# Decay matrices from differences of running sums, adaLN vectors of the first FFN by ScalarE products and GpSimd sums, and B kept once

## The chip, the cores and the metric

The kernel runs on one core of a Trainium2 chip. The metric is device microseconds of one execution; smaller is better.

## What is computed

The program is a block of two layers over 512 latent tokens and 256 context tokens of width 1024. Layer 0 runs grouped-query attention and a bidirectional Mamba-2 scan (SSD) side by side, layer 1 is a gated short convolution, and a SwiGLU FFN follows each. Before every sub-layer a normalized input is shifted and scaled, and its output is gated, by vectors that come from a conditioning vector `c`. The parts that the change touches, cut from the reference:

```python
mod = (silu(c) @ ada_w[i] + ada_b[i])[:, None, :]
sh1, sc1, g1, sh2, sc2, g2 = split(mod, 6, axis=-1)      # parts 0 .. 5

def segsum_exp(a):                                        # decay matrix of one chunk and head
    mask = tril(ones((l, l)))
    return exp(where(mask, a[..., :, None] - a[..., None, :], -inf))

a_cs = cumsum(dtc * a, axis=2)                            # running sums inside a chunk of 128
cb = einsum('bclgn,bcsgn->bcgls', cc, bc)
y_diag = einsum('bcgls,bgecls,bcsgep->bclgep', cb, segsum_exp(a_cs), xdt)
states = einsum('bclgn,bgecl,bclgep->bcgepn', bc, exp(a_cs[..., -1:] - a_cs), xdt)
y_off = einsum('bclgn,bgecl,cbgepn->bclgep', cc, exp(a_cs), h_in)
```

There are 4 latent and 2 context chunks, 2 groups of 4 heads and 2 directions. For a chunk and a group, the decay matrices of 4 heads and 2 directions are 2 x 4 matrices of 128x128.

## The kernel before

Activations lie with features on the 128 partitions and tokens along a row. A weight tile of 128x1024 is loaded into a buffer `wst` (three of them, `wp`, tag "wst"), split by ScalarE and VectorE into a high and a low part (`split`, L94 and L95), and multiplied in three passes (`mm3`, L116 to L118).

The change lies in `mixer`, in the stretch from about 145 us to 327 us of the profile. Two generators are stepped there in turns, one step of each per round: `ssd` (the scan) and `attention` (8 heads). The order of instructions on each engine comes from a scheduler of the tile framework, which may move an instruction past others of the program; each engine then runs its own list in order.

- The steps of `ssd` are four more column blocks of the input projection (`feature` with j = 6 to 9), with the recurrence of the chunk states beside them (`ssd_states` L652 and L656, `ssd_advance` L673 and L676), and then 8 units (`ssd_unit`), one for each chunk and group. A unit builds in PSUM `lp`, the exponents of the 2 x 4 decay matrices, and `ep`, the exponents of the running sums, spread over rows. ScalarE takes the exponentials (`lx` L767, `ce` L765), VectorE and GpSimd weigh and add them (L768, L770, L773, L774), and TensorE multiplies them with `xtok` and the states `hin` (L779, L780).
- The exponents are made from the step values themselves: GpSimd multiplies a triangular mask with the steps, as a high and a low part (`da`, L755, two buffers), and TensorE sums them by a product with another triangle (L757) and with a band (L758). So a unit has 2 matmuls for the mask (L751), 4 of L757 and 4 of L758.
- An attention head computes scores (L822), their exponentials (`ex`, L824) and the sum over values (L830). Ahead of it, for the next head, a first set of scores (L802) gives a maximum per row (`mx`, VectorE, L804), which ScalarE puts on a diagonal (`dm`, L805) and TensorE spreads (L808). The score tiles, the maximum tiles and `lp` share the two PSUM buffers `psS`.
- From the sixth round on, two steps a round, `ada_rest` computes parts 2, 3 and 4 of `mod` of layer 0 on VectorE: 24 loads of 512 KB into the `wst` buffers (L251), and for each two products with a column of `silu(c)`, added to a sum (L255 for the first, L257 for the others): 48 products for six halves of 512 columns, each half then transposed and reduced (L260, L261).
- `btok` holds B for each chunk and group twice side by side, so that one 128-row product yields both directions' states.

## Time and profile before

| | before |
|---|---|
| median of 3 runs | 1293.13 us (1292.08 to 1293.63) |
| the profiled execution | 1291.26 us |
| its span on the chip | 1289.4 us |
| TensorE (PE) busy | 1239.6 us, 96% of the span |
| VectorE (DVE) busy | 729.4 us, 57% |
| ScalarE (ACT) busy | 448.4 us, 35% |
| GpSimd (POOL) busy | 179.5 us, 14% |

The span runs from the first to the last instruction on the core; the execution's time has 1.9 us around it. Busy shares are means over the whole program. Matmuls are pipelined, and a record of one reaches past the start of the next, so that the busy time of TensorE overstates its work wherever it also waits.

### The profile page before, as it was taken

The page shows a single profiled execution, that of the slowest core. Times are in us where ns is not written, and L with a number is a line of the kernel's source. Part 1 is how long each engine was busy: PE and PEld are TensorE (multiplying, and loading weights), DVE is VectorE, ACT ScalarE, POOL GpSimd, SP SyncE. Part 2 cuts the span into 40 slices and gives each one's busy share as a digit, 9 for nine tenths or more (in the row PEclk, how much of TensorE's full clock was granted, in tenths as well). Part 3 has the DMA queues.
Part 4 walks back from the last instruction along what each step waited for, and adds up shares of the span by engine and source line. Part 5 has one row for each costly group of instructions (what it writes and reads, how often), then busy time and mean ns, then how long its engine had stood idle before and what let it go on. Part 6 is the DMA issues. An engine that isn't in the chain of part 4 may idle for free.

```text
span 1289.4 us, 15875 instructions
## 1 busy us (share of the span) xinstructions
PE 1239.6 (96%) x6086; PEld 1021.6 (79%) x6086; DVE 729.4 (57%) x1187; ACT 448.4 (35%) x675; POOL 179.5 (14%) x199
## 2 busy tenths in 40 slices
PE   5998988899999999999999999999999999999997
PEld 3887765567898888888888988888988888888886
DVE  4898799985564777788422554443743333332223
ACT  3534534455353222223222342223532222222221
POOL 3423335440220000000000100002200000000001
PEclk9999989999999999999999999999999999999998
DMA  9331343300514777777333323333133333333322
GB/s 369 127 99 49 96 155 125 115 17 1 163 50 143 227 243 243 235 240 249 118 91 94 111 79 93 95 97 112 50 114 98 99 98 98 97 91 90 94 87 66
DMA packets 54845, 158.52 MB, mean 123 GB/s; under 512 B 6000, under 2 KB 8688, under 8 KB 54512
## 3 DMA queue, kind: packets, MB, share of 16 engines
q1 hardware_dynamic: 54480, 157.20, 38.1%
q8 instruction: 48, 0.79, 0.2%
q10 hardware_dynamic: 288, 0.31, 0.1%
q14 instruction: 29, 0.24, 0.1%
HBM read 154.86 MB, written 2.10 MB: 122 GB/s over the span
## 4 chain that ended last, share of the span: by engine, by line
PE 83%; DVE 9%; DMA 3%; issue 3%; POOL 1%; ACT 0%; SPq 0%; DVEq 0%; ACTq 0%; POOLq 0%
PE psS L116 14%; PE psS L117 14%; PE psS L118 14%; PE psA L116 10%; PE psA L118 10%; PE psA L117 10%; DVE xtok L257 2%; PE psV L830 2%; DMA adaw<-ada 2%; PE psS L961 1%; PE psS L822 1%; DVE mx L804 1%; DVE wlo L95 1%; PE psS L963 1%; DMA xT<-xT 1%
## 5 line engine op out<-in xcount | busy, mean ns | idle before, releaser
L95 DVE TENSOR_TENSOR wlo<-wst,whi 128x1024 fp32r<-128x1024 f32 (+2 forms) x194 | 235.0, 1214 | 315.2 <-ACT whi L94 312.3
L94 ACT CAST whi<-wst 128x1024 fp32r<-128x1024 f32 (+2 forms) x194 | 198.2, 1025 | 544.8 <-PE psS L117 242.1
L116 PE MATMUL psS<-act_hi,whi 128*128 128x512 f32 x760 | 297.0, 391 | 1.2 <-DVE cs_a L573 1.0
L117 PE MATMUL psS<-act_lo,whi 128*128 128x512 f32 x760 | 296.7, 390 | 0.0
L118 PE MATMUL psS<-act_hi,wlo 128*128 128x512 f32 x760 | 296.6, 390 | 0.0
L118 PEld LDWEIGHTS psS<-act_hi,wlo 128*128 128x128 f32 x760 | 143.1, 188 | 29.7
L116 PEld LDWEIGHTS psS<-act_hi,whi 128*128 128x128 f32 x760 | 143.0, 188 | 29.5 <-issue 1.2
L117 PEld LDWEIGHTS psS<-act_lo,whi 128*128 128x128 f32 x760 | 143.0, 188 | 27.9
L325 POOL TENSOR_TENSOR sq_acc<-sq_acc,sq 128x512 f32<-128x512 f32 (+1 forms) x28 | 38.0, 1356 | 872.5 <-issue 645.8
L116 PE MATMUL psA<-ffn_h_hi,whi 128*128 128x512 f32 (+1 forms) x396 | 145.3, 367 | 0.0
L118 PE MATMUL psA<-ffn_h_hi,wlo 128*128 128x512 f32 (+1 forms) x396 | 144.9, 366 | 0.0
L117 PE MATMUL psA<-ffn_h_lo,whi 128*128 128x512 f32 (+1 forms) x396 | 144.8, 366 | 0.0
L257 DVE SCALAR_TENSOR_TENSOR ada_acc<-ada_st,silu_c,ada_acc 128x512 f32<-128x512 f32 x98 | 73.4, 749 | 27.5 <-DMA ada_st<-ada 26.0
L117 PEld LDWEIGHTS psA<-ffn_h_lo,whi 128*128 128x128 f32 x396 | 74.7, 189 | 12.1
L116 PEld LDWEIGHTS psA<-ffn_h_hi,whi 128*128 128x128 f32 x396 | 74.7, 189 | 12.0
L118 PEld LDWEIGHTS psA<-ffn_h_hi,wlo 128*128 128x128 f32 x396 | 74.7, 189 | 12.0
L116 PE MATMUL psA<-act_hi,whi 128*128 128x512 f32 (+1 forms) x216 | 80.0, 370 | 0.0
L118 PE MATMUL psA<-act_hi,wlo 128*128 128x512 f32 (+1 forms) x216 | 79.2, 367 | 0.8 <-DVE wlo L95 0.8
L117 PE MATMUL psA<-act_lo,whi 128*128 128x512 f32 (+1 forms) x216 | 79.5, 368 | 0.0
L916 DVE SCALAR_TENSOR_TENSOR xT<-psA,mod,xT 128x512 f32<-128x512 f32 (+1 forms) x40 | 25.7, 643 | 68.2 <-PE psA L118 68.0
L94 ACT CAST ffn_h_hi<-sg 128x512 fp32r<-128x512 f32 x44 | 27.4, 622 | 59.1 <-DVE sg L980 59.1
L118 PEld LDWEIGHTS psA<-act_hi,wlo 128*128 128x128 f32 x216 | 40.8, 189 | 8.0 <-DVE wlo L95 1.3
(297 smaller groups left out, 1804.4 us busy)
## 6 DMA issues: line engine op xcount, KB each, us to landing
wst<-w_gu SPq DMA_DIRECT2D x88, 512.0 KB, 3.6
ada_st<-ada SPq DMA_DIRECT2D x112, 256.0 KB, 4.0
wst<-w_dn SPq DMA_DIRECT2D x32, 512.0 KB, 3.5
wst<-ada SPq DMA_DIRECT2D x24, 512.0 KB, 3.8
wst<-w_sc SPq DMA_DIRECT2D x24, 512.0 KB, 3.6
adaw<-ada SPq DMA_DIRECT2D x16, 512.0 KB, 10.4
wst<-w_dn SPq DMA_DIRECT2D x16, 384.0 KB, 3.2
wst<-w_f SPq DMA_DIRECT2D x10, 512.0 KB, 3.6
```

Source lines behind the costliest of these rows:

```text
L94: nc.scalar.copy(hi, src)
L95: nc.vector.tensor_tensor(lo, src, hi.bitcast(F32), ALU.subtract)
L116: nc.tensor.matmul(out, lhsT=a[0], rhs=b[0], start=start, stop=False)
L117: nc.tensor.matmul(out, lhsT=a[0], rhs=b[1], start=False, stop=False)
L118: nc.tensor.matmul(out, lhsT=a[1], rhs=b[0], start=False, stop=stop)
L257: nc.vector.scalar_tensor_tensor(a, w[:, i], c, a, ALU.mult, ALU.add)
L325: nc.gpsimd.tensor_tensor(self.acc[:, ts], self.acc[:, ts], sq, ALU.add)
L804: nc.vector.tensor_reduce(mx[:, c:c + 1], s[:, 0:768], AX.X, ALU.max)
L822: nc.tensor.matmul(s[:, a * T:a * T + T], lhsT=kt[x][:, ks], rhs=q[x], start=(x == 0), stop=(x == 1))
L830: nc.tensor.matmul(av, lhsT=vz[:, kc, vs], rhs=e[:, a], start=(c + a == 0), stop=(c + a == CHUNKS - 1))
L916: nc.vector.scalar_tensor_tensor(xt[:, d, ts], ps, gate[:, d:d + 1], xt[:, d, ts], ALU.mult, ALU.add)
L961: nc.tensor.matmul(out, lhsT=a[:, k * P:(k + 1) * P], rhs=hi, start=(k == 0 and a is w[0]), stop=False)
```

## The change

It has three parts.

1. The decay matrices. `ssd_decay` keeps the running sums `acs` of the four latent chunks as a high and a low part (`rows`). `ssd_wide` transposes them once (`cols`: 128 rows, which stand for part, chunk, direction, group and head) and lets GpSimd make `wide` once, four copies of it, one for each head, that are zero in the other heads' rows. A unit takes differences of running sums by a product of a 0/1 selector `sel` with `wide` and one of `cols` with -1 (`neg`), beside the mask, and `ep` by one product of `band` with `wide`. A unit so has 7 matmuls of 512 columns in place of 10, and no `da` from GpSimd.
2. The vectors of the first FFN. Parts 3 and 4 (its shift and scale) go to a second `ada_rest` with `pair=True`: ScalarE multiplies each half of the `wst` buffer in place with the column of `silu(c)`, and GpSimd adds it to a sum in a tile of its own, `ada_more`. It starts with the second round, one step a round. Part 2 (the gate) stays on VectorE, one step a round.
3. `btok` holds B once. The two directions' states are two matmuls of 256 columns into 64 rows each, in place of one into 128 rows; the copies to `btok` are 2 in place of 6.

Some small setup moves with it: the masks are made ahead of the projection, and the constants grow by 84 columns.

```diff
@@ ada_rest
-    def ada_rest(self, pool, layer, parts, acc=None, bufs=2, tag=None):
+    def ada_rest(self, pool, layer, parts, acc=None, bufs=2, tag=None, pair=False, red=0):
...
                     for i in range(step):
                         c = self.sc[:, 0, k + i:k + i + 1]
-                        if k + i == 0:
+                        if pair:
+                            nc.scalar.activation(w[:, i], w[:, i], AF.Copy, scale=c)
+                            if k + i:
+                                nc.gpsimd.tensor_tensor(a, w[:, 0] if k + i == 1 else a, w[:, i], ALU.add)
+                        elif k + i == 0:
                             nc.vector.tensor_scalar(a, w[:, i], c, None, ALU.mult)
@@ mixer
+        self.ssd_masks(mp, sd)
...
-        self.ssd_masks(sm, sd)
+        self.ssd_wide(sm, sd)
...
-        ada = [self.ada_rest(None, 0, (2, 3, 4), (xtok[:, 0], xtok[:, 1]))]
+        more = mp.tile([P, T], F32, name="ada_more")
+        ada = [self.ada_rest(None, 0, (2,), (xtok[:, 0], xtok[:, 1]))]
+        other = [self.ada_rest(None, 0, (3, 4), (more, xtok[:, 1]), pair=True, red=4)]
...
+            if rounds > 0:
+                self.pump(1, other)
             if rounds > 5:
-                self.pump(2, ada)
+                self.pump(1, ada)
@@ to_tok
-            s = tp.rearrange("p c (g n) -> p c g n", g=2)
-            for c in range(nc_):
-                nc.scalar.copy(btok[:, c0 + c], s[:, c, :, None, :].broadcast_to([P, 2, 2, 64]))
+            nc.scalar.copy(btok[:, c0:c0 + nc_], tp.rearrange("p c (g n) -> p c g n", g=2))
@@ ssd_decay
-        self.split(dhi, dlo, dta)
+        self.split(rows[:, 0], rows[:, 1], acs[:, 2:6])
@@ ssd_wide (new)
+        nc.tensor.transpose(out=tp, in_=sd["rows"].rearrange("p a b c -> p (a b c)").bitcast(F32), identity=self.ident)
+        nc.vector.tensor_copy(cols, tp)
+        nc.gpsimd.tensor_tensor(wide, cols.bitcast(F32)[:, None, :].broadcast_to([P, 4, P]),
+                                sd["pos"][:, :, None].broadcast_to([P, 4, P]), ALU.mult)
@@ ssd_states
-            nc.tensor.matmul(st[:, lo:lo + n], lhsT=sd["btok"][:, c, g].rearrange("p a b -> p (a b)"),
-                             rhs=xw.rearrange("p a b c -> p (a b c)")[:, lo:lo + n], start=True, stop=True)
+                for c, e in ends:
+                    nc.tensor.matmul(st[64 * e:64 * e + 64], lhsT=sd["btok"][:, c, g], rhs=xw[:, e], start=True, stop=True)
@@ ssd_unit
-            nc.tensor.matmul(lp[:, e], lhsT=tri[:, 4], rhs=tri[:, 2 + e, None, :].broadcast_to([P, 4, P]),
+            nc.tensor.matmul(lp[:, e], lhsT=tri[:, 2], rhs=tri[:, e, None, :].broadcast_to([P, 4, P]),
                              start=True, stop=False)
-            for i, d in enumerate(sd["dta"]):
-                w = sp.tile([P, 4, P], F32R, name="da", tag="da", bufs=2)
-                nc.gpsimd.tensor_tensor(w, self.con(nm)[:, None, :].broadcast_to([P, 4, P]),
-                                        d[:, cc, hs, None].bitcast(F32).broadcast_to([P, 4, P]), ALU.mult)
-                nc.tensor.matmul(lp[:, e], lhsT=tri[:, e], rhs=w, start=False, stop=(i == 1))
-                nc.tensor.matmul(ep, lhsT=band[:, 64 - 64 * e:192 - 64 * e], rhs=w, start=(e == 0 and i == 0),
-                                 stop=(e == 1 and i == 1))
+            nc.tensor.matmul(lp[:, e], lhsT=sel[:, i, None].broadcast_to([P, P]), rhs=wide, start=False, stop=False)
+            nc.tensor.matmul(lp[:, e], lhsT=cols, rhs=neg[:, i, :, None].broadcast_to([P, 4, P]), start=False, stop=True)
+        nc.tensor.matmul(ep, lhsT=band[:, c, g], rhs=wide, start=True, stop=True)
```

What this does to the engines' lists is seen at three places. On TensorE, the fourth unit before (a row is a line, an operation, output<-inputs and shape; `ex,vz` is a head's sum over values, `kt,q` the tiles for its maximum):

```order
L751 MATMUL psS<-tri 128x512
L757 MATMUL psS<-da,tri 128x512 x2
L751 MATMUL psS<-tri 128x512
L830 MATMUL psV<-ex,vz 128x512 x2
L802 MATMUL psS<-kt_432,q_1976 128x512
L802 MATMUL psS<-kt_432,q_1976 128x256
L757 MATMUL psS<-da,tri 128x512
L758 MATMUL psA<-da,band 128x512
L757 MATMUL psS<-da,tri 128x512
L758 MATMUL psA<-da,band 128x512
```

and the same unit in the changed program:

```order
L798 MATMUL psA<-lx,xtok 128x256
L799 MATMUL psA<-ce,hin_803 128x256
L774 MATMUL psS<-tri 128x512
L776 MATMUL psS<-wide,sel 128x512
L777 MATMUL psS<-neg,cols 128x512
L774 MATMUL psS<-tri 128x512
L776 MATMUL psS<-wide,sel 128x512
L777 MATMUL psS<-neg,cols 128x512
L821 MATMUL psS<-kt_432,q_2019 128x512
```

The six matmuls of `lp` now stand together, and no other matmul has to fill the time in which GpSimd makes the next `da`; the one for `ep` stands further ahead.

On GpSimd, before, from the last states to the second unit's weighting (`xw` belongs to the states):

```order
L652 TENSOR_TENSOR xw<-xtok,sp_u 128x256 x2
L755 TENSOR_TENSOR da<-cons_446,dta_hi 128x512
L755 TENSOR_TENSOR da<-cons_446,dta_lo 128x512
L755 TENSOR_TENSOR da<-cons_446,dta_hi 128x512
L755 TENSOR_TENSOR da<-cons_446,dta_lo 128x512
L755 TENSOR_TENSOR da<-cons_446,dta_hi 128x512
L755 TENSOR_TENSOR da<-cons_446,dta_lo 128x512
L770 TENSOR_TENSOR lx<-lx,dt 128x512
```

and in the changed program, from there to the last unit's weighting:

```order
L676 TENSOR_TENSOR xw<-xtok,sp_u 128x256 x2
L257 TENSOR_TENSOR ada_more<-wst 128x512
L257 TENSOR_TENSOR ada_more<-ada_more,wst 128x512 x4
L789 TENSOR_TENSOR lx<-lx,dt 128x512
L257 TENSOR_TENSOR ada_more<-ada_more,wst 128x512 x2
L257 TENSOR_TENSOR ada_more<-wst 128x512
L789 TENSOR_TENSOR lx<-lx,dt 128x512
L257 TENSOR_TENSOR ada_more<-ada_more,wst 128x512 x6
L789 TENSOR_TENSOR lx<-lx,dt 128x512 x6
```

All 28 sums stand ahead of the third unit's weighting (14 of them in these rows, 14 earlier, between the `xw` and `hin` of the states), and nothing but the weighting follows.

On ScalarE, before, from the second unit's exponential of `lp` to the third's (`cbs`, `ce`, `lx` belong to units, `ex` and `dm` to heads):

```order
L767 ACTIVATE lx<-psS 128x1024
L765 ACTIVATE ce<-psA 128x512
L805 ACTIVATE dm<-cons_70,mx 128x128
L763 COPY cbs<-psA 128x128
L824 ACTIVATE ex<-psS 128x1024
L805 ACTIVATE dm<-cons_70,mx 128x128
L94 CAST act_hi<-ao 128x2x256
L767 ACTIVATE lx<-psS 128x1024
```

and in the changed program, the rows that end with the third unit's (`whi` is a weight's high part, L255 the new products):

```order
L255 ACTIVATE wst<-wst,silu_c 128x512 x2
L782 COPY cbs<-psA 128x128
L843 ACTIVATE ex<-psS 128x1024
L255 ACTIVATE wst<-wst,silu_c 128x512 x4
L782 COPY cbs<-psA 128x128
L824 ACTIVATE dm<-cons_70,mx 128x128
L843 ACTIVATE ex<-psS 128x1024
L94 CAST whi<-wst 128x1024
L824 ACTIVATE dm<-cons_70,mx 128x128
L784 ACTIVATE ce<-psA 128x512
L94 CAST act_hi<-ao 128x2x256
L786 ACTIVATE lx<-psS 128x1024
```

These are the last of the 32 products on ScalarE: all of them stand ahead of the third unit's exponentials, and each waits in its place for its load. On SyncE, which issues the loads, one of the 24 loads now stands ahead of each of the first two loads of the output projection's weights (`w_o`), and the other 22 follow; before, both `w_o` loads stood first.

## Rows read from the trace of the kernel before

**Rows 1.** Busy us by stretch: PE, PEld, DVE, ACT, POOL; clock, DMA share, GB/s.

```profile
145.00:196.00 51.00, 45.24 (x172) 32.14 (x172) 44.47 (x68) 18.22 (x29) 24.52 (x35) 0.93 0.46 144
196.00:224.00 28.00, 24.39 (x90) 15.02 (x88) 27.70 (x43) 12.15 (x22) 15.11 (x13) 1.00 0.35 112
224.00:283.00 59.00, 52.50 (x198) 35.35 (x199) 52.24 (x92) 29.22 (x49) 29.52 (x25) 0.97 0.26 80
283.00:327.00 44.00, 42.91 (x188) 30.29 (x188) 25.89 (x54) 21.55 (x35) 1.04 (x1) 1.00 0.00 1
```

**Rows 2.** Waits from 140 to 375 us: total us, times, longest.

```profile
ACT dm L805 <- DVE mx L804: 41.8, 25, 4.9
POOL da L755 <- PE psA L758: 22.9, 10, 8.2
POOL xw L652 <- PE psA L656: 22.5, 6, 14.3
...
PEld psS L802 <- DVE mx L804: 5.0, 5, 1.7
```

**Rows 3.** Groups on VectorE, GpSimd and ScalarE, 145 to 330 us: busy us, mean ns.

```profile
L257 DVE SCALAR_TENSOR_TENSOR xtok<-wst,silu_c,xtok 128x512 f32<-128x512 f32 x42 | 36.3, 865 | 2.7 <-DMA wst<-ada 2.2
L804 DVE TENSOR_REDUCE mx<-psS 128x1 f32<-128x768 f32 x32 | 30.2, 952 | 1.8 <-PE psS L802 1.1
...
L755 POOL TENSOR_TENSOR da<-cons,dta_lo 128x512 fp32r<-128x512 f32 x16 | 21.3, 1329 | 0.0
...
L755 POOL TENSOR_TENSOR da<-cons,dta_hi 128x512 fp32r<-128x512 f32 x16 | 18.0, 1126 | 41.1 <-PE psA L758 22.9 <-PE psS L757 17.4 <-PE psA L656 0.9
...
L255 DVE TENSOR_SCALAR xtok<-wst,silu_c 128x512 f32<-128x512 f32 x6 | 4.9, 824 | 0.9 <-DMA wst<-ada 0.9
...
L94 ACT CAST act_hi<-yu 128x512 fp32r<-128x512 f32 x4 | 2.5, 616 | 0.5 <-DVE yu L736 0.5
```

**Rows 4.** Groups of 224 to 283 us on TensorE and VectorE.

```profile
L830 PE MATMUL psV<-ex,vz 128*128 128x512 f32 x28 | 13.3, 596 | 0.1
L257 DVE SCALAR_TENSOR_TENSOR xtok<-wst,silu_c,xtok 128x512 f32<-128x512 f32 x13 | 11.3, 869 | 0.1
```

**Rows 5.** TensorE in order of time: start, us (x: instructions).

```profile
222.38 0.40 PE L757 MATMUL psS<-da,tri 128*128 128x512 f32 x1
...
223.07 0.40 PE L758 MATMUL psA<-da,band 128*128 128x512 f32 x1
...
270.08 1.88 PE L830 MATMUL psV<-ex,vz 128*128 128x512 f32 x4
271.79 0.59 PE L779 MATMUL psA<-lx,xtok 128*128 128x256 f32 x2
```

**Rows 6.** GpSimd sums of two full tiles, whole span, shapes apart.

```profile
L325 POOL TENSOR_TENSOR sq_acc<-sq_acc,sq 128x512 f32<-128x512 f32 x20 | 30.6, 1532 | 851.8 <-issue 645.8 <-ACT sq L322 205.9
```

**Rows 7.** SyncE in order of time, 130 to 260 us: the loads' issues.

```profile
145.99 97.18 SPq L251 DMA_DIRECT2D wst<-ada  x24
```

**Rows 8.** DMA issues on the page: KB each, us to landing.

```profile
wst<-ada SPq DMA_DIRECT2D x24, 512.0 KB, 3.8
```

**Rows 9.** ScalarE in order of time: exponentials of the third, fifth and eighth unit.

```profile
223.96 1.02 ACT L767 ACTIVATE lx<-psS 128x1024 f32<-128x1024 f32 x1
...
251.15 1.00 ACT L767 ACTIVATE lx<-psS 128x1024 f32<-128x1024 f32 x1
...
282.79 1.03 ACT L767 ACTIVATE lx<-psS 128x1024 f32<-128x1024 f32 x1 [0.48 <-PE psS L757]
```

**Rows 10.** VectorE in order of time, beside GpSimd work and without.

```profile
207.01 2.70 DVE L773 SCALAR_TENSOR_TENSOR lx<-lx,dt 128x128 f32<-128x128 f32 x4
...
218.97 1.09 DVE L773 SCALAR_TENSOR_TENSOR lx<-lx,dt 128x128 f32<-128x128 f32 x4
219.99 0.95 DVE L804 TENSOR_REDUCE mx<-psS 128x1 f32<-128x768 f32 x1
```

**Rows 11.** GpSimd in order of time at the first of these.

```profile
207.45 1.05 POOL L755 TENSOR_TENSOR da<-cons,dta_hi 128x512 fp32r<-128x512 f32 x1 [2.26 <-PE psA L758]
```

More of the change, by code (lines that the diff above doesn't have):

```diff
@@ L402, in mixer @@
         nc.sync.dma_start(out=self.rows, in_=t["rows"])
-        for x, pool in ((1, mp), (2, pp)):
+        for x, pool in ((1, pp), (2, pp)):
             self.cons.append(pool.tile([P, CAT[x + 1] - CAT[x]], F32, name=f"cons{x}"))
@@ L450, in mixer @@
         xtok = sm.tile([P, CHUNKS, T], F32, name="xtok")
-        btok = sm.tile([P, CHUNKS, 2, 2, 64], F32, name="btok")
+        btok = sm.tile([P, CHUNKS, 2, 64], F32, name="btok")
         sd = {"xtok": xtok, "btok": btok, "hin": [sm.tile([P, 512], F32, name=f"hin{c}") for c in range(4)]}
         self.ssd_decay(mp, dt, sd)
+        self.ssd_masks(mp, sd)
         cw = sm.tile([P, 24], F32, name="half_conv")
@@ L501, in mixer @@
             alive = (next(a, 1) is None) or alive
+            if rounds > 0:
+                self.pump(1, other)
             if rounds > 5:
-                self.pump(2, ada)
+                self.pump(1, ada)
             rounds += 1
         self.pump(1000, ada)
+        self.pump(1000, other)
         apm.__exit__(None, None, None)
@@ L623, in ssd_decay @@
         nc.vector.tensor_tensor(wd, wd, dt, ALU.mult)
-        dhi = mp.tile([P, CHUNKS, 16], F32R, name="dta_hi")
-        dlo = mp.tile([P, CHUNKS, 16], F32R, name="dta_lo")
-        self.split(dhi, dlo, dta)
-        sd.update(wd=wd, dec=dec, dta=(dhi, dlo))
+        rows = mp.tile([P, 2, 4, 16], F32R, name="sum_rows")
+        self.split(rows[:, 0], rows[:, 1], acs[:, 2:6])
+        sd.update(wd=wd, dec=dec, rows=rows)
     def ssd_masks(self, mp, sd):
         nc = self.nc
-        tri = mp.tile([P, 6, P], F32R, name="tri")
@@ L638, in ssd_masks @@
-        nc.vector.tensor_copy(tri[:, 4], self.ident)
-        nc.vector.tensor_copy(tri[:, 5], one)
-        nc.vector.tensor_scalar(band[:, 0:128], one, 0.0, None, ALU.mult)
-        nc.vector.tensor_scalar(band[:, 128:192], one[:, 0:64], 0.0, None, ALU.mult)
-        nc.vector.tensor_copy(band[:, 64:128], one[:, 0:64])
-        sd.update(tri=tri, band=band)
-    def ssd_states(self, sp, sd, c, dirs, tag):
+        for e, x in enumerate((ge, le)):
+            nc.vector.tensor_tensor(tri[:, e], x, self.ident, ALU.subtract)
+            nc.vector.tensor_scalar(tri[:, e], tri[:, e].bitcast(F32), NEG, None, ALU.mult)
@@ new lines, in ssd_masks @@
+        nc.vector.tensor_copy(tri[:, 2], self.ident)
+        nc.vector.tensor_copy(tri[:, 3], one)
+        sel = mp.tile([P, 16], F32R, name="sel")
+        nc.vector.tensor_copy(sel, self.con("sel", 16))
+        neg = mp.tile([P, 16, 4], F32R, name="neg")
+        nc.vector.tensor_copy(neg, self.con("neg", 64).rearrange("p (a b) -> p a b", b=4))
+        pos = mp.tile([P, 4], F32, name="pos")
+        nc.vector.tensor_copy(pos, self.con("pos", 4))
+        sd.update(tri=tri, sel=sel, neg=neg, pos=pos)
@@ new lines, in ssd_wide @@
+    def ssd_wide(self, mp, sd):
+        nc, sel = self.nc, sd["sel"]
+        tp = self.psA((P, P))
+        nc.tensor.transpose(out=tp, in_=sd["rows"].rearrange("p a b c -> p (a b c)").bitcast(F32), identity=self.ident)
+        cols = mp.tile([P, P], F32R, name="cols")
+        nc.vector.tensor_copy(cols, tp)
+        wide = mp.tile([P, 4, P], F32R, name="wide")
+        nc.gpsimd.tensor_tensor(wide, cols.bitcast(F32)[:, None, :].broadcast_to([P, 4, P]),
+                                sd["pos"][:, :, None].broadcast_to([P, 4, P]), ALU.mult)
+        band = mp.tile([P, 4, 2, P], F32R, name="band")
+        for g in range(2):
+            nc.scalar.copy(band[:, :, g].rearrange("p c (e n) -> p c e n", e=2),
+                           sel.bitcast(F32).rearrange("p (c e g) -> p c e g", e=2, g=2)[:, :, :, g, None].broadcast_to([P, 4, 2, 64]))
+        sd.update(band=band, cols=cols, wide=wide)
@@ L646, in ssd_states @@
+    def ssd_states(self, sp, sd, ends, tag):
         nc = self.nc
@@ L649, in ssd_states @@
             xw = sp.tile([P, 512], F32, name="xw", tag=tag, bufs=2).rearrange("p (a b c) -> p a b c", a=2, b=4)
-            st = self.psA()
-            for e in dirs:
+            st = self.psA((P, 256))
+            for c, e in ends:
                 nc.gpsimd.tensor_tensor(
@@ L654, in ssd_states @@
                     sd["wd"][:, c, 8 * e + 4 * g:8 * e + 4 * g + 4, None].broadcast_to([P, 4, 64]), ALU.mult)
-            lo, n = 256 * dirs[0], 256 * len(dirs)
-            nc.tensor.matmul(st[:, lo:lo + n], lhsT=sd["btok"][:, c, g].rearrange("p a b -> p (a b)"),
-                             rhs=xw.rearrange("p a b c -> p (a b c)")[:, lo:lo + n], start=True, stop=True)
-            for e in dirs:
-                r = slice(64 * e, 64 * e + 64)
-                out.append((g, e, st[r, 256 * e:256 * e + 256]))
+            with self.tc.manual_schedule(engines={mybir.EngineType.PE}):
+                for c, e in ends:
+                    nc.tensor.matmul(st[64 * e:64 * e + 64], lhsT=sd["btok"][:, c, g], rhs=xw[:, e], start=True, stop=True)
+                    out.append((g, e, st[64 * e:64 * e + 64]))
         return out
@@ L741, in ssd_unit @@
         nc, tc = self.nc, self.tc
-        hin, xtok, tri, band = (sd[n] for n in ("hin", "xtok", "tri", "band"))
+        hin, xtok, tri, band, sel, neg, cols, wide = (sd[n] for n in ("hin", "xtok", "tri", "band", "sel", "neg", "cols", "wide"))
         hin = hin[c]
@@ L1115, in _layout @@
     con[:, at + 128:at + 256] = ge
+    con[q, at + 256 + q // 4 % 16] = 1.0
+    con[q, at + 272 + q % 4] = 1.0
+    con[q, at + 276 + q % 64] = -1.0
     at = CAT[2]
```

27 lines of the change are left out of this document (12 added, 15 removed).

## The prediction

> **What bounds the kernel now.** First the page: TensorE is busy nearly everywhere, so only a stretch in which it also waits can give time back. The table of busy time by stretch shows one. From 145 to 283 us, where the scan's states and units run beside attention, TensorE is recorded busy for 122.1 of 138 us and VectorE for 124.4 [rows 1]; from 283 to 327, when the units are over, TensorE is busy for 42.9 of 44. In the first part it is VectorE that is full: 27.7 of 28 us from 196 to 224.
>
> Next the waits, to see whether that reaches TensorE. ScalarE's `dm` waits 41.8 us in 25 pieces for the maximum `mx`, and TensorE's own weight loads into the array (PEld) wait for `mx` as well, because a maximum's scores hold one of the two `psS` buffers [rows 2]. A maximum itself takes 0.95 us [rows 3]; the rest of its delay is that it stands in VectorE's list behind other work, and 48 rows of that are the products of `ada_rest` at 0.87 and 0.82 us, 41.2 us in all. So `mx`, and with it the score and decay tiles, is late on account of `ada_rest`. The other chain is GpSimd's: `da` waits 22.9 us for the matmuls that read its two buffers, and those wait for it in turn.
>
> **The change part by part.** The sum is made in two stretches that are limited by different things, with the profiled execution's 1291.3 us as its base; the median of the runs is 1.9 higher.
>
> VectorE loses 32 of the 48 products, 28 x 0.865 + 4 x 0.824 = 27.5 us [rows 3]. ScalarE gains 32 products of 128x512 between SBUF tiles. It has no such row before; the nearest, a cast of that size, takes 0.62 us, so 19.8 us. In these stretches ScalarE is busy for 59.6 of 138 us [rows 1], so its sum has room; its order may not (below). The copies of `band` and the fewer ones of `btok` cancel to within 1 us.
>
> GpSimd loses 32 rows of `da`, 21.3 + 18.0 = 39.3 us, and gains 28 sums. The nearest row is a sum of two full tiles of that size, 1.53 us [rows 6]; `da`, with a broadcast input, took 1.13 and 1.33. So 28 x 1.53 = 42.9 us (31.6 at 1.13), and 1 for `wide`. Its total hardly changes, but it moves ahead: all of it now stands before the third unit.
>
> TensorE loses 24 matmuls of 512 columns. Records overlap, so the cost is the distance of starts: three steps in 0.69 us, 0.23 each [rows 5], 5.5 us in all. The states' matmuls keep their columns, 20 of 256 where there were 4 of 512 and 12 of 256. I take nothing for them; a loss of 2 us if each of the 20 cost 0.1 more is the other end.
>
> What is moved costs nothing by these covers: the masks and selectors are as many small rows of VectorE as before, the first weights of `w_o` are issued behind one load each and are not read until attention is at its last head, and the constants' 84 columns ride on a load that is there. If the `w_o` split were late all the same, it would hold its buffer longer, which is the case of slow loads below.
>
> *Units four to eight, from 223.96 to 282.79* (exponentials of the third and eighth unit [rows 9]): 58.8 us, 11.8 a unit. In 224 to 283 VectorE is busy for 52.2 of 59 us, of which 13 products are 11.3 [rows 4]; as the order shows, nearly all of them go or move ahead, and VectorE is left with about 41. GpSimd has one row a unit left. What TensorE must do there is bounded from its rows: 198 matmuls [rows 1], of which 28 take 1.71/4 = 0.43 [rows 4, 5] and 170 at most 0.23: 12.0 + 39.1 = 51.1, less 15 x 0.23 = 47.7. That is a bound from above, since many of the 170 have fewer columns; at 0.20 on average it is 43. I take 48 us: no wait left by the upper count, about 4 us of waits by the lower. So **-11**, between -15.7 (by 43) and -6, which is five units at the 10.5 us of the last three: these ran from 251.15 to 282.79 [rows 9], when VectorE had no products left.
>
> *From 145 to the third unit.* VectorE is relieved here too, but now the loads decide. Each buffer is held for a load of 3.8 us [rows 8], then for two products of VectorE, 1.7, or for a product of ScalarE and two sums, 0.6 + 3.1. With 14 of the last 22 loads of the second sort, that is 6.8 us on average, and 2.3 us a load with three buffers; before, 24 loads were issued in 97.2 us, 4.05 each [rows 7], while VectorE was full. I take 3.2, halfway. The 22 start when GpSimd has made the second sum between the context's states, about 152 (a reading of the order, with the first issue before at 146); 152 + 22 x 3.2 + 1.2 for the last two products gives 223.6, where the third unit's exponentials stood before, at 224.0. So **0**. At 2.3 it would be 203.8, but GpSimd then caps it: its 39.6 us in 145 to 224 [rows 1] become some 67 (less the 12 `da` of three units at 1.23, plus 27 sums and `wide`), so no more than 12 us can be won. At 4.05 it is +18 later.
>
> The sums on GpSimd may also slow VectorE: four weighted sums of VectorE took 2.70 us beside a `da`, and 1.09 without [rows 10, 11]. But 39.3 us of `da` leave as 42.9 us of sums come, and `mx`, which reads PSUM, kept its 0.95 us [rows 10]; I take nothing for it, and 3.6 us of loss as the other end. A rule of the Trainium skill speaks against the change here: the page "SBUF — State Buffer", section "Who interferes with whom", has VectorE and GpSimd share a port pair under an exclusive lock, so that one of the two fully blocks. The trace agrees for sums of SBUF tiles, at 2.70 against 1.09 us. By the rule every sum holds a row of VectorE for its length, as every `da` did, and the change would be worth 3.6 us less, 1286 on the medians; by the rows the chain through `mx` is exempt.
>
> The sum: -11 + 0 = **-11**, 1280.3 on the profiled execution's scale, **1282** on that of the medians.
>
> **The rivals.**
>
> *ScalarE waits for loads.* Its products stand in its list ahead of `dm`, `ex` and `ce`, and a late load holds all of these. If the loads keep the old 4.05 us, because a buffer now also waits for GpSimd, the third unit is 18 us late, and -11 leaves +7: 1300. It decides from 3.7 us a load (11 us / 22 = 0.5 above mine). For it: nearly all rows of ScalarE and TensorE behind are in order. Against it: VectorE, which made the old pace, is relieved.
>
> *GpSimd takes VectorE's place.* If its old 22.5 us of waits of `xw` for TensorE [rows 2] come on top of the 67, the third unit comes at 145 + 89.5 = 234.5, 10.5 late, and the change is 0: 1293. The page "GPSIMD Engine Reference" of the Trainium skill, section "Engine selection", has two-input sums on GpSimd about half as fast as on VectorE, and would leave the sums where they were. The trace agrees on the speed, 1.53 us against 0.87 for a product with a sum, but not yet on the outcome, since GpSimd had 39.4 us free in 145 to 224 [rows 1]; hence the small chance.
>
> *The units don't get faster than 10.5 us*, because the two `psS` buffers, not VectorE, set their pace: -6: 1287. For it: the pace of 251 to 283; against it: there GpSimd still made `da`.
>
> *Both stretches gain.* The loads run at 2.8 us and TensorE's work is the smaller count: -9 and -15: 1269. For it: TensorE's 15.9 us without a record in 145 to 283; against it: GpSimd's 67 us in the first part.
>
> **How the numbers follow.** Chances: the forecast 0.50, the slower units 0.15, both gain 0.13, GpSimd 0.10, ScalarE's loads 0.12. A measurement tells this kernel from no change at about 0.2%, 2.6 us. The first three are faster, 0.78; GpSimd's case is the same, 0.10; the loads' case slower, 0.12. The range 1270 to 1295 runs from the case in which both gain to beyond no change, and leaves out most of the slowest case and a part of the fastest. The forecast's own range is 1277 to 1286.
>
> **What the profile of the changed kernel would show.** Right: VectorE clearly under nine tenths from 224 on, `mx` no longer named in waits of TensorE's PEld, the third unit's exponential of `lp` at about 224 and the eighth's at about 272, the stretch from there to the first FFN as long as before, and everything behind it shifted alone. Wrong: gaps of TensorE before `dm` or `ex` rows that stand behind a ScalarE product which waits for a load; GpSimd without a pause to 230; or units that keep 10.5 us with VectorE idle. The prediction fails if the loads take 3.7 us or more each, or if the new order puts states and heads so that TensorE waits for GpSimd's `xw` in the first stretch.

## Result and the profile after

The changed kernel takes 1299.55 us (median; 1299.42 to 1301.72), against 1292.61 (1288.95 to 1293.63) for the kernel before on the same chip: ratio 1.0064, 95% interval 1.0045 to 1.0083. It is slower by some 8 us. The prediction was 1282 us, in a range of 1270 to 1295, with 0.12 for slower.

The profiled execution took 1299.49 us with a span of 1297.7, 8.3 us more than before. Its busy time by stretch, the same stretches as [rows 1] (busy us of each engine, with its instructions in brackets; then TensorE's granted clock as a share of full speed, the share of DMA time, and GB/s):

```profile
145.00:196.00 51.00, 39.30 (x150) 25.27 (x151) 33.53 (x44) 25.55 (x43) 39.62 (x47) 0.88 0.45 133
196.00:224.00 28.00, 24.20 (x84) 14.03 (x82) 25.15 (x39) 19.34 (x33) 15.03 (x13) 0.92 0.62 203
224.00:283.00 59.00, 51.33 (x191) 34.30 (x192) 44.88 (x85) 31.63 (x52) 13.11 (x11) 0.97 0.12 40
283.00:327.00 44.00, 42.48 (x182) 29.31 (x181) 28.17 (x60) 24.36 (x39) 1.04 (x1) 0.96 0.00 1
```

Over the whole span TensorE is busy for 1239.4 us (96%), VectorE for 710.0, ScalarE for 468.6 and GpSimd for 179.1. VectorE was relieved, as planned: from 44.5 to 33.5 us in the first stretch. But TensorE lost 5.9 us there (45.2 to 39.3), where it had been slack already. The ends of the third and eighth unit and of the last head's sum are read from ScalarE's timeline (start, length, line, output<-input):

```profile
233.72 1.02 ACT L786 ACTIVATE lx<-psS 128x1024 f32<-128x1024 f32 x1
283.39 1.02 ACT L786 ACTIVATE lx<-psS 128x1024 f32<-128x1024 f32 x1 [0.73 <-PE psS L777]
335.36 0.58 ACT L862 COPY as<-psV 64x512 f32<-64x512 f32 x1 [6.71 <-PE psV L849]
```

Against [rows 9] the third unit is 9.8 us late, and the eighth 0.6: the five units between took 49.7 us in place of 58.8. The last head's sum was read at 326.95 before, and is 8.4 us late. So there are three terms, +9.8, -9.2 and +7.8, and they are seen best when the stretches are cut at these three points. First the kernel before, then the changed one; the fourth row of each is the whole:

```profile
145.00:223.96 78.96, 69.63 (x260) 47.16 (x259) 72.14 (x110) 30.34 (x51) 39.59 (x48) 0.96 0.42 133
223.96:282.79 58.83, 52.29 (x197) 35.17 (x198) 52.09 (x91) 29.05 (x48) 29.57 (x25) 0.97 0.26 80
282.79:326.95 44.16, 43.06 (x188) 30.44 (x187) 26.09 (x55) 21.71 (x35) 1.04 (x1) 1.00 0.00 1
145.00:326.95 181.95, 164.99 (x644) 112.78 (x644) 150.31 (x254) 81.09 (x132) 70.19 (x73) 0.97 0.27 84
```

```profile
145.00:233.72 88.72, 71.57 (x262) 44.77 (x263) 68.21 (x97) 52.44 (x88) 62.42 (x64) 0.90 0.50 155
233.72:283.39 49.67, 43.64 (x163) 29.19 (x162) 35.35 (x71) 24.08 (x40) 5.34 (x5) 0.97 0.06 21
283.39:335.36 51.97, 50.45 (x209) 34.50 (x208) 28.17 (x60) 25.39 (x41) 1.04 (x1) 0.97 0.00 1
145.00:335.36 190.36, 165.66 (x632) 108.46 (x633) 131.72 (x227) 101.92 (x167) 68.81 (x70) 0.94 0.25 78
```

The first part grew at almost the same number of matmuls (260, 262): TensorE's time without a record went from 9.3 to 17.2 us, and the clock from 0.96 to 0.90. In the last part there is no wait to speak of (50.45 of 51.97, 43.06 of 44.16); it is longer because 209 matmuls stand there and not 188, at a clock of 0.97 in place of 1.00. So much of the second and the third term is the same work: 34 matmuls fewer stand in the five units, and 21 more behind them. The heads' work that no longer stands among the units has to be done after them. Over the whole, TensorE is busy as long as before, 165.7 against 165.0 us, with 12 records fewer, and its gaps went from 17.0 to 24.7 us.

Where TensorE waits in the first part is told by the waits from 143 to 224 us (engine, line, what it waited for: us in total, times, longest):

```profile
ACT wst L255 <- DMA wst<-ada: 11.4, 7, 3.6
POOL ada_more L257 <- ACT wst L255: 10.9, 4, 3.2
DVE xtok L261 <- DMA wst<-ada: 8.2, 5, 3.3
PE psS L841 <- DVE mx L823: 6.8, 3, 5.0
ACT wst L255 <- POOL ada_more L257: 4.3, 1, 4.3
PE psA L681 <- POOL xw L676: 3.9, 2, 3.3
```

Each of the three engines that share the `wst` buffers now waits for the others or for a load, and TensorE again for `mx`. Before, VectorE waited 3.1 us for loads [rows 3]. The longest wait of TensorE, from the timelines of VectorE, ScalarE, TensorE and the load queue (in square brackets the idle time ahead and what ended it):

```profile
183.03 3.55 DVE L261 SCALAR_TENSOR_TENSOR xtok<-wst,silu_c,xtok 128x512 f32<-128x512 f32 x2 [2.07 <-DMA wst<-ada]
190.64 2.67 DVE L261 SCALAR_TENSOR_TENSOR xtok<-wst,silu_c,xtok 128x512 f32<-128x512 f32 x2 [3.29 <-DMA wst<-ada]
193.34 1.82 DVE L823 TENSOR_REDUCE mx<-psS 128x1 f32<-128x768 f32 x2
186.60 7.54 SPq L251 DMA_DIRECT2D wst<-ada  x4
186.81 0.86 PE L821 MATMUL psS<-kt,q 128*128 128x512 f32 x4
192.02 1.33 ACT L255 ACTIVATE wst<-wst,silu_c 128x512 f32<-128x512 f32 x2 [4.26 <-POOL ada_more L257]
194.36 0.80 PE L841 MATMUL psS<-q,kt 128*128 128x512 f32 x1 [4.97 <-DVE mx L823]
194.95 0.63 PE L841 MATMUL psS<-q,kn 128*128 128x512 f32 x1
195.38 0.63 PE L841 MATMUL psS<-q,kt 128*128 128x512 f32 x1
```

VectorE makes two products from 183.0 to 186.6, at 1.8 us each; a load is issued as they end, at 186.60, into the buffer that they give back; the next product stands ahead of `mx` in VectorE's list and starts at 190.64, when it has landed. The loads behind VectorE's other two long waits (2.07 us to 183.03, 1.56 us to 197.32) were likewise issued as a product of VectorE ended, at 179.22 and 193.34. So 6.9 of its 8.2 us are waits for the buffer that VectorE itself had held last, while ScalarE and GpSimd had the other two; only in the last two, 0.5 and 0.8 us, had a sum of GpSimd held it. The scores of `mx` had been ready since 187.7, and TensorE stood 5.0 us. Behind this wait its rows are 0.43 us apart, where rows of that size at the full clock are 0.23 apart [rows 5]: it runs at the lower of its two levels for a while (granted clock 0.50 from 194 to 196 us). Prices in the changed kernel from 145 to 336 us, by group (busy us, mean ns; idle before them):

```profile
L257 POOL TENSOR_TENSOR ada_more<-ada_more,wst 128x512 f32<-128x512 f32 x24 | 33.1, 1378 | 12.1 <-ACT wst L255 10.9
L823 DVE TENSOR_REDUCE mx<-psS 128x1 f32<-128x768 f32 x32 | 30.3, 953 | 5.2 <-PE psS L821 4.8
L255 ACT ACTIVATE wst<-wst,silu_c 128x512 f32<-128x512 f32 x30 | 20.2, 716 | 20.0 <-DMA wst<-ada 11.4 <-POOL ada_more L257 4.3 <-DVE mx L823 2.9
L261 DVE SCALAR_TENSOR_TENSOR xtok<-wst,silu_c,xtok 128x512 f32<-128x512 f32 x14 | 17.5, 1253 | 8.4 <-DMA wst<-ada 8.2
```

### The profile page after: what moved, and what is told of

The parts are those of the page before. It is cut to its first block, busy times and chain, and to the rows that moved or that the text cites. A ratio compares the mean times of both kernels' runs of the same rounds, so it can differ in the third digit from the quotient of the medians.

```text
span 1297.7 us, 15831 instructions
## 1 busy us (share of the span) xinstructions
PE 1239.4 (96%) x6073; PEld 1017.3 (78%) x6073; DVE 710.0 (55%) x1160; ACT 468.6 (36%) x705; POOL 179.1 (14%) x196
## 4 chain that ended last, share of the span: by engine, by line
PE 83%; DVE 7%; DMA 4%; issue 2%; ACT 2%; POOL 1%; SPq 0%; DVEq 0%; POOLq 0%; ACTq 0%
PE psS L116 14%; PE psS L117 14%; PE psS L118 14%; PE psA L116 10%; PE psA L117 10%; PE psA L118 10%; PE psV L849 2%; DMA wst<-ada 2%; DMA adaw<-ada 2%; PE psS L980 1%; PE psS L841 1%; DVE wlo L95 1%; DVE xtok L261 1%; DVE mx L823 1%; PE psS L982 1%
## 5 line engine op out<-in xcount | busy, mean ns | idle before, releaser
L849 PE MATMUL psV<-ex,vz 128*128 128x512 f32 x96 | 48.8, 633 | 1.2 <-ACT ex L843 1.2
```

The source lines that it names most:

```text
L849: nc.tensor.matmul(av, lhsT=vz[:, kc, vs], rhs=e[:, a], start=(c + a == 0), stop=(c + a == CHUNKS - 1))
```

## The experiments

"Against before" is the ratio to the kernel before of the same call, with its 95% interval, and in us at 1292; "gaps" is the time without a record of TensorE from 145 us to the last head's sum, worked out from the busy times by stretch as above, and "clock" the granted clock there. The last three columns are those of the one profiled execution, which lies within some 2 us of the kernel's median, but 4.8 us above it in e12 and 4.2 us in e11.

| kernel | median us | ratio to before (interval) | us | last sum | gaps | clock |
|---|---|---|---|---|---|---|
| changed | 1299.55 | 1.0064 (1.0045 to 1.0083) | +8.3 | 335.36 | 24.7 | 0.94 |
| e1_products_back | 1287.16 | 0.9962 (0.9949 to 0.9974) | -4.9 | 323.26 | 17.3 | 0.96 |
| e2_old_decay | 1300.77 | 1.0074 (1.0059 to 1.0089) | +9.6 | 335.98 | 21.0 | 0.94 |
| e6_states_alone | 1292.66 | 1.0007 (0.9997 to 1.0016) | +0.9 | 327.85 | 17.7 | 0.96 |
| e3_vector_last | 1293.50 | 1.0014 (1.0006 to 1.0023) | +1.8 | 327.34 | 20.8 | 0.94 |
| e4_none_on_vector | 1303.08 | 1.0095 (1.0082 to 1.0109) | +12.3 | 338.25 | 28.1 | 0.91 |
| e8_last_third | 1287.37 | 0.9966 (0.9954 to 0.9978) | -4.4 | 324.15 | 17.2 | 0.96 |
| e9_vector_first | 1288.63 | 0.9983 (0.9975 to 0.9992) | -2.2 | 322.65 | 17.7 | 0.97 |
| e10_few_sums | 1289.60 | 0.9990 (0.9979 to 1.0000) | -1.3 | 324.86 | 16.8 | 0.94 |
| e11_sums_on_vector | 1289.90 | 0.9993 (0.9980 to 1.0007) | -0.9 | 329.90 | 18.5 | 0.93 |
| e12_sums_alone | 1295.34 | 1.0043 (1.0027 to 1.0058) | +5.6 | 336.30 | 22.2 | 0.91 |
| e13_no_shift_scale | 1280.38 | 0.9918 (0.9905 to 0.9931) | -10.6 | 317.83 | 11.5 | 0.96 |
| e15_states_on_vector | 1303.69 | 1.0087 (1.0073 to 1.0102) | +11.2 | 337.63 | 23.3 | 0.91 |
| e16_sums_of_other_data | 1291.66 | 1.0003 (0.9989 to 1.0016) | +0.4 | 325.38 | 16.6 | 0.94 |
| e17_idle_sums | 1295.78 | 1.0027 (1.0016 to 1.0037) | +3.5 | 329.79 | 19.5 | 0.93 |

The scheduler orders each kernel anew, so that a few us between two of them can also be order; the main readings below rest on differences of 4 us or more, or on rows, and smaller ones are worth no more than a hint.

**The parts of the change.** The products back on VectorE:

```diff
-        ada = [self.ada_rest(None, 0, (2,), ...)]
-        other = [self.ada_rest(None, 0, (3, 4), ..., pair=True, red=4)]
+        ada = [self.ada_rest(None, 0, (2, 3, 4), (xtok[:, 0], xtok[:, 1]))]
...
-            if rounds > 0:
-                self.pump(1, other)
             if rounds > 5:
-                self.pump(1, ada)
+                self.pump(2, ada)
```

> The products of the first FFN's shift and scale go back to VectorE (48 products, two steps a round after the sixth, as in the kernel before); decay matrices, states and B stay new. Theory A (the time is lost by the split of the products: VectorE's 16 remaining products stand in order ahead of the maxima and wait for loads that share three buffers with ScalarE's and GpSimd's, 8.2 us of waits, and take 1.25 us each beside GpSimd's sums instead of 0.75): both go, so the first head ends at 191 us again instead of 200, and 32 `da` rows fewer also leave VectorE alone; 1284 to 1290 us. Rival B (the time is lost by the states' 40 smaller matmuls, the transposed sums and `wide` ahead of the first head, 4 us of TensorE by 155 us): the first head stays 4 us or more late, 1294 to 1300 us.

The decay matrices back (`ssd_decay`, `ssd_masks` and the ten matmuls of a unit as before, no `ssd_wide`), and the kernel before with the states alone:

```diff
@@ e6: before, with
-        btok = sm.tile([P, CHUNKS, 2, 2, 64], F32, name="btok")
+        btok = sm.tile([P, CHUNKS, 2, 64], F32, name="btok")
...
+                for c, e in ends:
+                    nc.tensor.matmul(st[64 * e:64 * e + 64], lhsT=sd["btok"][:, c, g], rhs=xw[:, e], start=True, stop=True)
@@ e2: e6, with ada_rest, ada and other of the changed kernel
```

> The decay matrices are made as before (32 `da` rows of GpSimd, 24 more matmuls); states and B are new, and the products are split between VectorE and ScalarE with GpSimd as in the changed kernel. Theory A: the split alone costs what it cost, and GpSimd has sums and `da` rows, so the units lose as well: 1300 to 1310 us. Rival B: without the transposed sums and `wide` most of the loss goes: 1290 to 1296 us.

> The kernel before with only B kept once and the states by matmuls of 64 columns of weights, both directions in one call. Theory A: within 2 us of the kernel before, 1291 to 1295 us. Rival B: 2 to 5 us slower, 1295 to 1298 us, with the first head late by that much.

The states cost nothing that can be measured (+0.9). With them, the decay matrices bring the kernel to -4.9, the split of the products alone to +9.6. So rival B falls, and the split of the products is the loss. The kernel with the products back is faster than both. Its stretches, cut at its own third unit, eighth unit and last sum:

```profile
145.00:218.51 73.51, 66.44 (x260) 42.28 (x257) 65.31 (x106) 30.82 (x51) 25.43 (x36) 0.95 0.44 136
218.51:274.28 55.77, 46.61 (x165) 30.34 (x164) 51.03 (x94) 25.64 (x41) 6.67 (x5) 0.94 0.30 94
274.28:323.26 48.98, 47.93 (x205) 33.07 (x204) 26.49 (x56) 25.36 (x40) 1.04 (x1) 1.00 0.00 1
145.00:323.26 178.26, 160.97 (x628) 105.69 (x625) 142.83 (x255) 81.82 (x132) 33.13 (x42) 0.96 0.28 86
```

TensorE's busy time falls by 4.0 us, 165.0 to 161.0, while its gaps stay (17.0, 17.3): by this the gain is the matmuls that were removed. The eighth unit comes 8.5 us earlier and the last sum 3.7: the rest is given back behind the units, at 98% of TensorE.

**Where the products stand.**

```diff
@@ e3: VectorE's products behind the others, in one queue
+        other = [..., *ada]
...
             if rounds > 0:
                 self.pump(1, other)
@@ e4: none on VectorE
+        other = [self.ada_rest(None, 0, (2, 3, 4), (more, xtok[:, 1]), pair=True)]
...
+                self.pump(1 + rounds % 2, other)
@@ e8: one queue; the last third on ScalarE and GpSimd
+        ada = [self.ada_rest(None, 0, (2, 3), ...), self.ada_rest(None, 0, (4,), ..., pair=True, red=4)]
@@ e9: one queue; VectorE's third first
+        ada = [self.ada_rest(None, 0, (2,), ...), self.ada_rest(None, 0, (3, 4), ..., pair=True, red=4)]
...
             if rounds > 5:
                 self.pump(2, ada)
```

> The changed kernel with VectorE's 16 products put behind ScalarE's and GpSimd's in one queue, one step a round from the second round on; the rest of them comes after the loop. Theory A: VectorE waits for no load before 200 us, so the first head ends some 5 us earlier than in the changed kernel and TensorE's wait of 5.0 us for a maximum goes; 1288 to 1295 us unless the products left at the end stand before the first projection. Rival C (it is ScalarE's products, ahead of the exponentials and waiting for loads, that hold TensorE, not VectorE's): the first head stays at 200 us, 1297 to 1302 us.

> All 48 products of shift, scale and gate on ScalarE with their 42 sums on GpSimd, none on VectorE, one and two steps in turn a round from the second on. Theory A (what cost most was VectorE's products waiting for loads ahead of the maxima and running beside GpSimd's sums): VectorE has neither, `mx` comes at once, but 42 sums of 1.3 us are 55 us on GpSimd and the third unit's states stand behind them; 1286 to 1293 us. Rival C (ScalarE's products hold the exponentials, GpSimd's sums hold `xw`, and these cost the time): worse than the changed kernel, 1300 to 1310 us.

> As the kernel with the products back on VectorE (1287.2 us), but the last third of them, 16 products, goes to ScalarE with 14 sums on GpSimd, in one queue behind the other two thirds, so that no two consumers' loads mix. Theory A: VectorE never waits behind another engine's load, and units four to eight, which took 55.8 us with the products back, lose up to half of their VectorE products; 1282 to 1287 us. Rival C: ScalarE's waits for loads ahead of exponentials cost as much wherever they stand: 1288 to 1293 us.

> The changed kernel's split, but one queue: VectorE's 16 products first from the seventh round on, ScalarE's and GpSimd's 32 behind them, two steps a round. Theory A: the first head ends by 193 us, since neither engine has products behind the other's loads before it, and 1283 to 1290 us. Rival C: the time moves with the products to the third to sixth head, 1292 to 1300 us.

In e3 VectorE's products wait 0.2 us in place of 8.4 and take 0.81 us in place of 1.25, and 6.5 of the 13.2 us between the changed kernel and e1 come back:

```profile
L261 DVE SCALAR_TENSOR_TENSOR xtok<-wst,silu_c,xtok 128x512 f32<-128x512 f32 x14 | 11.3, 806 | 0.2
```

That spoke for theory A, but e4 refutes it as the whole: with no product on VectorE at all, and 16 products and 14 sums more on ScalarE and GpSimd, the kernel loses the most, +12.3, with 28.1 us of gaps. So ScalarE's products and GpSimd's sums ahead of the third unit cost time by themselves, and VectorE's waits are one way in which it shows. Begun late, the same split (e9) costs 2.7 us against e1, and a split of the last third alone (e8) nothing that can be measured. Nowhere does it gain.

**ScalarE or GpSimd.**

```diff
@@ e10: few sums
-                            if k + i:
+                            if k + i == 1:
@@ e11: sums on VectorE
-                                nc.gpsimd.tensor_tensor(a, w[:, 0] if k + i == 1 else a, w[:, i], ALU.add)
+                                nc.vector.tensor_tensor(a, w[:, 0] if k + i == 1 else a, w[:, i], ALU.add)
@@ e12: sums alone
-                            nc.scalar.activation(w[:, i], w[:, i], AF.Copy, scale=c)
@@ e13: no loads, products or sums of parts 3 and 4
...
+        nc.gpsimd.memset(more, 0.0)
```

> Leaves out 24 of GpSimd's 28 sums (the shift and the scale of the first FFN then miss six of eight parts); everything else as in the changed kernel. Theory A: VectorE's products take 0.75 us instead of 1.25, 7 us, and the buffers come free sooner, so the loads and VectorE's waits for them are shorter; half or more of the 8 us between the changed kernel and the one before goes: 1288 to 1295 us. Rival C (ScalarE's products and the loads alone): less than 2 us goes, 1297 to 1300 us.

> The changed kernel with its 28 sums on VectorE instead of GpSimd; ScalarE's 32 products stay. Theory D (the sums on GpSimd cost the time: they hold the load buffers 1.3 us each, slow VectorE's products from 0.75 to 1.25 us, and stand ahead of `xw`): without them VectorE has 28 sums of 0.75 us more than in the changed kernel, but no waits of TensorE for `xw`; 1288 to 1294 us. Rival C (ScalarE's products ahead of the exponentials, with their waits for loads): 1296 to 1303 us, since nothing of that is taken away.

> Leaves out ScalarE's 32 products (the shift and the scale of the first FFN are then sums of unscaled weights); the loads, GpSimd's 28 sums and everything else as in the changed kernel. Theory D: GpSimd's sums alone keep most of the cost, 1295 to 1299 us. Rival C: most of it goes with ScalarE's products, 1286 to 1291 us.

> Leaves out the loads, products and sums of the first FFN's shift and scale altogether (zeros are reduced instead). It is the floor for any placing of these products. If VectorE's products cost the kernel with the products back (1287.2 us) its units: 1274 to 1281 us, a floor 6 us or more below. If TensorE's own matmuls set the stage once the decay matrices are changed, as its 161 us of busy time of 178 there suggest: 1282 to 1287 us, so that no placing can win more than 5 us.

Without 24 of GpSimd's 28 sums (e10), or with all of them on VectorE (e11), 9.6 and 9.2 us go, though ScalarE's products and their waits for loads stay: 14.0 and 10.9 us of such waits against 11.4 in the changed kernel.

```profile
L255 ACT ACTIVATE wst<-wst,silu_c 128x512 f32<-128x512 f32 x29 | 19.4, 714 | 16.0 <-DMA wst<-ada 14.0 <-DVE mx L823 2.0
L255 ACT ACTIVATE wst<-wst,silu_c 128x512 f32<-128x512 f32 x30 | 20.4, 715 | 11.1 <-DMA wst<-ada 10.9
```

(e10 first, then e11.) The sums alone (e12) keep 10.5 of the 13.2 us over e1, though VectorE's products wait 3.5 us for loads there in place of 8.5. So it is GpSimd's sums; ScalarE's products cost 2.7 to 4.0 us (changed kernel less e12, e11 less e1). The floor without any of it (e13) is 5.7 us under e1 and 10.6 under the kernel before, so a placing could have given 11 only by costing nothing at all. Its stretches show why:

```profile
145.00:219.19 74.19, 67.00 (x259) 42.44 (x256) 61.82 (x102) 33.80 (x54) 26.69 (x36) 0.95 0.30 93
219.19:264.28 45.09, 42.27 (x165) 28.79 (x164) 30.84 (x66) 23.87 (x40) 5.20 (x5) 1.00 0.00 0
264.28:317.83 53.55, 52.05 (x209) 35.68 (x208) 28.17 (x60) 25.36 (x41) 1.04 (x1) 0.94 0.00 1
```

The five units take 45.1 us, 13.7 less than before, with VectorE busy for 30.8 of them; but the stretch behind them is 9.4 us longer than before.

**How the sums cost it.** Three ways were open: `xw` and `hin` stand behind sums on GpSimd; a sum keeps the load buffer until it has read it; and VectorE's rows run longer beside a sum.

```diff
@@ e15: xw (L676) and hin (L695) on VectorE
-                nc.gpsimd.tensor_tensor(
+                nc.vector.tensor_tensor(
@@ e16: the changed kernel, sums of a ready tile (still = bf)
-                                nc.gpsimd.tensor_tensor(a, w[:, 0] if k + i == 1 else a, w[:, i], ALU.add)
+                                nc.gpsimd.tensor_tensor(a, still if k + i == 1 else a, still, ALU.add)
@@ e17: e1, with
+                for k in range(1, KC):
+                    nc.gpsimd.tensor_tensor(more, bf if k == 1 else more, bf, ALU.add)
...
```

> The changed kernel with the small products of the states (`xw`, 24 rows, and the running `hin`, 18 rows or so) on VectorE instead of GpSimd; GpSimd keeps its 28 sums. It tells apart how the sums cost the time. Theory D1 (by the queue: `xw` and `hin` stand behind sums on GpSimd, and TensorE and the states wait for them): these waits go, the first head ends at 191 to 195 us, 1288 to 1293 us. Rival D2 (by what they do to VectorE: its rows run longer beside a sum, and its products wait for the buffers that the sums hold): nothing of that goes, and VectorE has some 15 us of rows more; 1297 to 1305 us.

> The changed kernel, but GpSimd's 28 sums add a tile that lies ready (`bf`) instead of ScalarE's products, so that they wait for no load and hold no load buffer; a buffer is free after ScalarE's two products. The shift and the scale of the first FFN are then sums of other data. Theory E1 (held buffers: loads come late and VectorE's and ScalarE's products wait for them): those waits shrink from 19.8 us to a few and the time goes to 1288 to 1292 us. Rival E2 (VectorE's rows run longer beside a sum): 1295 to 1300 us.

> The kernel with the products back on VectorE (1287.2 us) with 28 sums of a ready tile added on GpSimd, two a round from the second round on, whose result nobody reads; nothing waits for them, but `xw` stands behind some of them. Theory E1 (held buffers): no buffer is held by them, so 1286 to 1289 us. Rival E2: VectorE's products go from 0.80 us towards 1.1 to 1.3 us while the sums run, 10 us or so of VectorE ahead of the third unit, and the time to 1291 to 1297 us.

e15 got slower still, +11.2, with the first head's sum at 200.1 as in the changed kernel (200.3): D1 falls as stated, but not cleanly, since VectorE also has 20.3 us of rows more. e16 doesn't settle it: `xw` stands behind sums as before, and TensorE's weight loads wait 7.0 us for it against 6.1 in the changed kernel, but its matmuls only 0.7 against 3.9.

e16 shows that it matters what the sums read: only that was changed, and +8.3 became +0.4. GpSimd still makes its sums, but they hold no load buffer and wait for no product. The loads come faster, the last 21 of them issued in 54.9 us, 2.6 each, where the changed kernel needs 3.15, and VectorE's products wait for 1.7 us in place of 8.2. ScalarE's waits for loads stay, 13.8 us, against the expectation. First the changed kernel's loads, then VectorE's products in e16 and in e10, and e16 from 145 us to its third unit:

```profile
152.61 69.22 SPq L251 DMA_DIRECT2D wst<-ada  x22
L261 DVE SCALAR_TENSOR_TENSOR xtok<-wst,silu_c,xtok 128x512 f32<-128x512 f32 x14 | 13.8, 989 | 1.9 <-DMA wst<-ada 1.7
L261 DVE SCALAR_TENSOR_TENSOR xtok<-wst,silu_c,xtok 128x512 f32<-128x512 f32 x14 | 13.5, 964 | 3.1 <-DMA wst<-ada 2.9
145.00:228.36 83.36, 71.08 (x260) 44.25 (x261) 67.18 (x103) 52.40 (x87) 59.31 (x60) 0.90 0.56 177
```

That e16 gains by the buffers alone isn't shown. VectorE's products are shorter there as well, 0.99 us in place of 1.25, and hardly longer than in e10, which makes 4 sums. Over all rows of VectorE from 145 us to the third unit, what they take beyond the shortest row of their kind in the same trace is 7.8 us in e16 and 12.6 in the changed kernel, an estimate from the rows. And the first head's sum ends at 200.2 as in the changed kernel: the wait of 5.0 us for `mx` is gone, but others stand in its place, and e16 gains only behind that head, 5.4 us up to the third unit and 4.6 in the units.

e17 shows the longer rows: sums that hold nothing and that nobody waits for cost e1 8.4 us (-4.9 to +3.5). The products of VectorE, e1 first, then e17 with its first stretch:

```profile
L261 DVE SCALAR_TENSOR_TENSOR xtok<-wst,silu_c,xtok 128x512 f32<-128x512 f32 x42 | 33.4, 795 | 4.1 <-DMA wst<-ada 3.4
```

```profile
L261 DVE SCALAR_TENSOR_TENSOR xtok<-wst,silu_c,xtok 128x512 f32<-128x512 f32 x42 | 41.0, 976 | 4.7 <-DMA wst<-ada 3.9
145.00:232.17 87.17, 73.44 (x256) 45.49 (x253) 78.12 (x110) 32.86 (x55) 61.72 (x59) 0.84 0.39 121
```

The third unit comes 13.7 us later than in e1, and VectorE is busy for 12.8 us more ahead of it, 78.1 of 87.2 us against 65.3 of 73.5: it is as full as there, with longer rows. By the same estimate 9.3 us of it are what the rows take beyond their shortest (13.8 against 4.5); the products alone take 29.8 us (29 rows) against 22.8 (28). GpSimd's queue is not the way here, though `xw` stands behind these sums too: TensorE's matmuls wait 1.5 us for it, as in e1 (1.6), and its weight loads 4.4 against 2.3. So longer rows cost time by themselves where VectorE is full. How the 8.3 us of the changed kernel divide between them, the held buffers and GpSimd's queue is not shown: e16 takes a part of all three away at once.

## Why the prediction was wrong

*What bounds the kernel*: that VectorE holds TensorE through `mx` was right, and so was that only a stretch in which TensorE waits can give time back. But I read the units as the stage's end. They are not: the heads are, and behind the eighth unit TensorE is busy for 97 or 98% in the kernel before, the changed one, e1 and e13 alike.

*"The stretch from there to the first FFN as long as before"* failed: +7.8 us, 44.2 to 52.0. It shows alone in e1 and e13, where the eighth unit is 8.5 and 18.5 us earlier and the last sum 3.7 and 9.1. Gains of the units are worth about half, and only as far as they remove matmuls or gaps of TensorE over the whole stage.

*Units four to eight, -11* (-15.7 to -6): -9.2. The size came out, the mechanism only in part. VectorE went from 52.1 of 58.8 us to 35.4 of 49.7, as forecast, but TensorE's gaps only from 6.5 to 6.0 us. The stretch is shorter because 34 matmuls fewer stand there: 15 of them, three a unit, were removed, as the sum had it; the other 19 are, by the counts, work that the forecast had left among the units and that came behind them. Against e1, with the same matrices and 48 products on VectorE, relief does show: the five units take 55.8 us there, with gaps of 9.2 against 6.0.

*From 145 to the third unit, 0* failed: +9.8 us. The load pace, on which it rested, was right: 22 loads in 69.2 us, 3.15 each, against 3.2. But a pace says nothing of who waits for each load: VectorE's own products, in order ahead of `mx`, waited 8.2 us for loads, 6.9 of them for the one buffer that VectorE could turn round while ScalarE and GpSimd had the other two, where I had counted the holding time as an average over both sorts of loads. Nor is the third unit tied to the loads' end: ScalarE's last product is done at 227.6, and its exponentials come 6.1 us later, behind VectorE's rows. The total of GpSimd was no limit: it was busy for 62.4 of 88.7 us there.

*"I take nothing for it, and 3.6 us of loss as the other end"*, for VectorE's rows beside GpSimd's sums, failed. Its 14 weighted sums took 1.25 us each, where the same operation takes 0.75 later in the same run, 7 us in all; `mx`, which reads PSUM, kept its 0.95. `da` was replaced by sums of about the same length, but these now stand beside VectorE's products and the states, and not beside the units. What that costs depends on VectorE's room: in e17, where VectorE is full, it is 8.4 us. The rule of the Trainium skill that I set aside ("SBUF — State Buffer", section "Who interferes with whom") has a VectorE row with two SBUF inputs contend with a GpSimd row that reads SBUF, and a reduction not; the trace agrees on both, 1.25 against 0.75 us and 0.95.

*Prices.* ScalarE's product was forecast at 0.62 us and took 0.72, 22.9 us for 32 against 19.8. GpSimd's sums were forecast at 1.53 and took 1.38. TensorE's 24 matmuls at 5.5 us: its busy time fell by 4.0 in e1, over all of the stage. The states at nothing: +0.9 us in e6, within the uncertainty.

*The rival "ScalarE waits for loads", 1300 us*, has the time and not the mechanism: its loads of 4.05 us did not come, and with ScalarE's waits for loads as long as ever e10 and e16 lose the 8 to 10 us. Its place, TensorE's gaps behind rows that wait for a load, and the clause that a buffer now also waits for GpSimd were right; the row that waits is VectorE's as well as ScalarE's.

*The rival "GpSimd takes VectorE's place"* has the third unit nearly right, 234.5 against 233.7, by accident: the 22.5 us that `xw` waited for TensorE are gone from the waits of the changed kernel. The sign of failure named last did come, though: TensorE's matmuls wait 3.9 us for `xw` in the first stretch, against 1.1 before.

Left open: how much of the changed kernel's lower clock (0.90 ahead of the third unit) is a loss of its own. e10 has the same 632 records as the changed kernel in 163.1 us of busy time, 2.6 less, at the same 0.90 and 0.94; a kernel with these gaps and the full clock wasn't made. In e17 TensorE's records ahead of the third unit take 7.0 us more than in e1 for 4 fewer, at 0.84 in place of 0.95. Open too is what holds the first head's sum at 198 to 200 us in e10, e11 and e16, against 191.9 in e1. A kernel with more load buffers, the plain test of the held buffers, wasn't made.
